# The four running sums of a Strassen pair move into four PSUM tiles, with weight buffers of their own

## The chip, the cores and the metric

The kernel runs on one core of one Trainium2 chip. The metric is the device time of one execution in microseconds; the number for a kernel is the median of its runs.

## The reference, cut to what matters

The reference computes one step of a two-layer decoder for 512 prompt tokens and 64 sample tokens (576 columns, kept transposed: features on the partitions, tokens along the free dimension). Each layer is a mixer with an input and an output projection, then a squared-ReLU MLP, then a gated embedding. The change touches the MLP of the second layer, and through shared PSUM space the stages on both sides of it:

```python
def channel_mixer(h, norm_g, w_up, w_down):
    a = jax.nn.relu(rmsnorm(h, norm_g) @ w_up)
    return h + (a * a) @ w_down
```

with `w_up` 1024 x 4096 and `w_down` 4096 x 1024, all in float32.

## The kernel before, in words

**Products.** A weight arrives as a unit of 128 x 512 floats (256 KB, four 128 x 128 blocks). ScalarE rounds it to a high part (`whi`, a cast, L92), VectorE takes the rest (`wlo`, a subtraction, L93); activations are split likewise. A product is then three matmuls of 128 x 288 columns: high by high, high by low, low by high. 576 columns make two halves of 288, `lo` and `hi`. `pieces` (L128) is the plain linear map: 24 matmuls for each unit and both halves, into a PSUM tile `[128, 2, 512]` of the pool `big`.

**The MLP of the second layer** is `ffn_quad` (L305). Its 32 output tiles of the up projection are made as four `plain` ones (L336) and 14 `pair`s (L344). A pair makes two tiles at once by a Strassen scheme (Winograd's form): seven products of 12 matmuls in place of eight, into four running sums X, Z, Y and V. Their order is the tuple `plan` in `quad` (L175): X from b11, Z from t1, Y from t2, again X from b21, again Y from t3, V from t4, again Z from b22. The operands t1 to t4 are sums of activations, made once by `operands` (L317) while the plain tiles run; the sums of weights (`qsum`, L160) are made on VectorE for each pair. Between the products VectorE and ScalarE read the running sums: `L350` copies X, `L352` reads Y, `L354` reads X again, `L356` reads Y again, `L357` and `L361` read Z, `L359` reads V. Each pair's results go through ReLU, square and a scale, and are split into `hidh` and `hidl`. After every two pairs eight `back` products (L370, "down" in the trace, 24 matmuls each) add their part of the down projection to the residual h on VectorE (L372); while the pairs j run, the downs of the two before are made, four to a pair.

**PSUM.** `banks(3, 2)` (L63) opens a pool of three `big` tiles and two small ones, from the second norm of layer 0 to the end. A pair takes two `big` tiles: X and Y are the halves of one, `qa`, Z and V those of the other, `qb`:

```python
al = self.big.tile([128, 2, 512], F32, name="qa", tag="big")
be = self.big.tile([128, 2, 512], F32, name="qb", tag="big")
X, Y, Z, V = al[:, 0, 0:HT], al[:, 1, 0:HT], be[:, 0, 0:HT], be[:, 1, 0:HT]
```

**Buffers in SBUF.** All splits of weights, for pairs and for everything else, come from one ring of three `whi` and three `wlo`. Raw weights of a pair (`qraw`) have eight buffers, their sums four.

**What sets the order.** Nothing is ordered by hand at these places. The program is written in the order of the functions above; a scheduler then orders each engine's instructions and sets a semaphore wait wherever two instructions of different engines touch the same tile. Each engine takes its list strictly in that order; loads of weights wait in the list of SyncE.

Of the kernel before, what the change touches and what calls it, by code (L numbers as in the profile page):

```python
# [6 lines left out]
F32 = mybir.dt.float32  # L7
# [9 lines left out]
HT = 288  # L17
KU = 4
NTS = [128, 603]
QRAW, QSUM, PLAIN = 8, 4, 2  # L20
EPS = 1e-6
# [11 lines left out]
def f(ap):  # L33
    return ap.bitcast(F32)
# [7 lines left out]
class Net:  # L42
# [43 lines left out]

    def split_unit(self, raw):
        nc, kt = self.nc, raw.shape[1]
        ps = [128, KU, 128]
        hi = self.wp.tile([128, kt, 128], F32R, name="whi", tag="whi", padded_shape=ps)  # L90
        lo = self.wp.tile([128, kt, 128], F32R, name="wlo", tag="wlo", padded_shape=ps)
        nc.scalar.copy(hi, raw)  # L92
        self.lo.tensor_sub(lo, raw, f(hi))  # L93
        return hi, lo
# [52 lines left out]
    def quad_units(self, s1, s2):  # L147

        nc = self.nc
        ps = [128, KU, 128]  # L150
        n = s1.shape[1] // 2
        raws = []
        for s, a in ((s1, 0), (s2, 0), (s2, n), (s1, n)):
            raw = self.qp.tile(ps, F32, name="qraw", tag="qraw", bufs=QRAW)
            self.last = nc.sync.dma_start(raw, s[:, a:a + n])
            self.flush(self.share)
            raws.append(raw)
        a11, a21, a22, a12 = raws

        def add(a, b):  # L160
            o = self.qp.tile(ps, F32, name="qsum", tag="qsum", bufs=QSUM)
            nc.vector.tensor_add(o, a, b)
            return o

        yield a11
        u1 = add(a21, a22)
        yield u1
        u2 = add(u1, a11)
        yield u2
        yield a12  # L170
        yield add(a11, a21)
        yield a22
        yield add(u2, a12)

    def quad(self, s1, s2, B):  # L175


        al = self.big.tile([128, 2, 512], F32, name="qa", tag="big")
        be = self.big.tile([128, 2, 512], F32, name="qb", tag="big")
        X, Y, Z, V = al[:, 0, 0:HT], al[:, 1, 0:HT], be[:, 0, 0:HT], be[:, 1, 0:HT]  # L180
        mm = self.nc.tensor.matmul
# [3 lines left out]
        for o, b, first in plan:  # L185
            hi, lo = self.split_unit(next(us))
            n = len(B[b])
# [8 lines left out]
    def split(self, x, pool=None, tag="x"):  # L196
# [3 lines left out]
        lo = pool.tile([128, T], F32R, name=tag + "l", tag=tag + "l")  # L200
        self.nc.scalar.copy(hi, x)
        self.nc.vector.tensor_sub(lo, x, f(hi))
        return hi, lo
# [101 lines left out]
def ffn_quad(N, h, xs, up, down, after, psrc, gain):  # L305
# [3 lines left out]
    with tc.tile_pool(name="qw", bufs=2, reuse_waits="tile") as qp, \  # L309
# [3 lines left out]
        N.quad_pools(qp)  # L313
        lo, hi = slice(0, HT), slice(HT, T)
        B = {n: [] for n in ("b11", "b21", "b22", "t1", "t2", "t3", "t4")}

        def operands(k):  # L317
# [11 lines left out]
            ph, pl = N.split(p, qx, "qx")  # L329
            qh, ql = N.split(q, qx, "qx")  # L330
            cut = lambda t, s: (t[0][:, s], t[1][:, s])
            for n, t, s in (("b11", xs[k], lo), ("b21", xs[k + 4], lo), ("b22", xs[k + 4], hi), ("t1", (ph, pl), lo),
# [11 lines left out]
        def pair(m):  # L344
            s = ft.tile([128, 2, HT], F32, name="qs", tag="qs")
            a = ft.tile([128, T], F32, name="fa", tag="fa")
            b = ft.tile([128, T], F32, name="fb", tag="fs")
            g = N.quad(up[m], up[m + 1], B)
            X = next(g)
            nc.scalar.copy(s[:, 0], X)  # L350
            Z, Y = next(g), next(g)
            nc.vector.tensor_sub(s[:, 1], s[:, 0], Y)  # L352
            next(g)
            nc.scalar.activation(a[:, lo], X, AF.Relu)  # L354
            next(g)
            nc.vector.tensor_sub(s[:, 0], s[:, 0], Y)  # L356
            nc.vector.scalar_tensor_tensor(b[:, hi], Z, -1.0, s[:, 0], op0=MUL, op1=SUB)  # L357
            V = next(g)
            nc.vector.tensor_sub(b[:, lo], V, s[:, 0])  # L359
            next(g)  # L360
            nc.vector.tensor_add(a[:, hi], Z, s[:, 1])  # L361
            nc.scalar.activation(b, b, AF.Relu)
# [14 lines left out]
        for j in range(16):  # L377
# [7 lines left out]
            else:  # L385
                hid[j // 2] += pair(2 * j)
            if j == 15:
# [1332 lines left out]
def trunk(tc, I, O):  # L1720
    with ExitStack() as ctx:
# [19 lines left out]
        with N.banks(2, 4):  # L1741
# [13 lines left out]
            xs = N.norm_end(acc)  # L1755
            layer0(N, h, xs, I, O, V, lambda m: N.norm_tile(h[m], col("norm_ffn0", m)))
        ctx.enter_context(N.banks(3, 2))
        xs = N.norm_end()
        with tc.tile_pool(name="s5pre", bufs=1, reuse_waits="tile") as pool:
            pre = s5_pre(N, pool, I, D)  # L1760
            p = ffn(N, h, xs, I["up0"], I["down0"], lambda m: N.norm_tile(h[m], col("norm_pe0", m)), I["p0"],
                    lambda: (next(pre, None), next(pre, None)))
            for _ in pre:
                pass
        xs = N.norm_end()
        N.norm_begin()
        pe(N, h, xs, I["gate0"], I["proj0"], p, lambda m: N.norm_tile(h[m], col("norm_mix1", m)), True)
        xs = N.norm_end()
        layer1(N, h, xs, I, O, V, D, lambda m: N.norm_tile(h[m], col("norm_ffn1", m)))
        xs = N.norm_end()  # L1770
        p = ffn_quad(N, h, xs, I["up1"], I["down1"], lambda m: N.norm_tile(h[m], col("norm_pe1", m)), I["p1"],
                     lambda m: col("norm_ffn1", m))
        xs = N.norm_end()
# [42 lines left out]
```

## Time and profile before

| | |
|---|---|
| median of 3 runs | 1589.25 us (1587.27 to 1590.63) |
| the profiled execution's own time | 1587.57 us |
| its span | 1585.8 us |
| TensorE busy | 1473.8 us, 93% |
| VectorE busy | 951.5 us, 60% |
| ScalarE busy | 593.6 us, 37% |

The profiled execution took 1.8 us more than its span, and 1.7 us less than the median. TensorE is the engine that the others feed. Its matmuls overlap each other, so its busy time hides short stops; how far the starts of matmuls lie apart tells more than their lengths. The pairs of `ffn_quad` fill the span from 1084.56 to 1468.09 us.

### The profile page before, as it was taken

Reading aid. Unit: us, or ns where it says so; the run is one execution under the profiler, and the core shown is the slowest. Engines: PE = TensorE matmul, PEld = TensorE weight load, DVE = VectorE, ACT = ScalarE, POOL = GpSimd, SP = SyncE. Lnnn points to the kernel's source line nnn. Section 1 sums busy time; section 2 is a strip of 40 time slices with the busy share of each in tenths; the row PEclk is TensorE's granted clock in tenths of the full one; section 3 lists DMA queues with packets and bytes.
Section 4 is the critical chain, followed back from the end, with each engine's and each line's share of the span. In section 5 each row is a group of like instructions: output and inputs, shape, how many; then the busy total and the mean of one; then the engine's idle time right before and its main releaser. Section 6 shows DMA issues by size and latency. Waiting matters only on the chain. (4 is left out here: it accounts for less than half of the span.)

```text
span 1585.8 us, 27284 instructions
## 1 busy us (share of the span) xinstructions
PE 1473.8 (93%) x10687; PEld 1428.8 (90%) x10687; DVE 951.5 (60%) x1680; ACT 593.6 (37%) x1121; POOL 430.2 (27%) x689
## 2 busy tenths in 40 slices
PE   7999999998989899999999997998989899998996
PEld 6889899788989899999999987997989888898996
DVE  6757455589834224454336785677666666665655
ACT  5462363223222112223334512544434343444552
POOL 4644253234868544510111151020000000000212
PEclk9998999999989999999999996997999999999998
DMA  5121112252322333363222754341222222221222
GB/s 195 57 74 48 38 54 84 89 151 68 122 75 91 95 102 102 100 174 105 81 76 80 256 149 130 91 133 54 80 74 81 80 80 68 80 75 39 78 85 73
DMA packets 107281, 149.46 MB, mean 94 GB/s; under 512 B 30800, under 2 KB 46544, under 8 KB 107152
## 3 DMA queue, kind: packets, MB, share of 16 engines
q1 hardware_dynamic: 78960, 128.63, 26.1%
q10 hardware_dynamic: 27616, 16.99, 3.9%
q8 instruction: 84, 1.38, 0.4%
q0 software_dynamic: 576, 2.10, 0.3%
q14 instruction: 45, 0.37, 0.1%
HBM read 130.73 MB, written 16.43 MB: 93 GB/s over the span
## 5 line engine op out<-in xcount | busy, mean ns | idle before, releaser
L92 ACT CAST whi<-wraw 128x512 fp32r<-128x512 f32 (+2 forms) x352 | 211.8, 605 | 531.9 <-PE down L121 142.8
L93 DVE TENSOR_TENSOR wlo<-wraw,whi 128x512 fp32r<-128x512 f32 (+1 forms) x306 | 222.7, 729 | 200.8 <-ACT whi L92 194.2
L120 PE MATMUL down<-hidh,whi 128*128 128x288 f32 x1024 | 306.2, 299 | 12.9 <-ACT whi L92 12.9
L122 PE MATMUL down<-hidh,wlo 128*128 128x288 f32 x1024 | 306.0, 299 | 0.0
L121 PE MATMUL down<-hidl,whi 128*128 128x288 f32 x1024 | 303.2, 296 | 0.0
L228 POOL TENSOR_TENSOR acc<-acc,sq 128x576 f32<-128x576 f32 x45 | 69.0, 1533 | 747.7 <-ACT sq L227 729.4
L120 PEld LDWEIGHTS down<-hidh,whi 128*128 128x128 f32 x1024 | 194.7, 190 | 16.5 <-ACT whi L92 16.5
L121 PEld LDWEIGHTS down<-hidl,whi 128*128 128x128 f32 x1024 | 195.9, 191 | 0.0
L122 PEld LDWEIGHTS down<-hidh,wlo 128*128 128x128 f32 x1024 | 193.9, 189 | 0.2 <-DVE wlo L93 0.2
L120 PE MATMUL up<-xh,whi 128*128 128x288 f32 x576 | 172.7, 300 | 8.2 <-ACT whi L92 8.0
L122 PE MATMUL up<-xh,wlo 128*128 128x288 f32 x576 | 171.8, 298 | 2.5 <-DVE wlo L93 2.5
L121 PE MATMUL up<-xl,whi 128*128 128x288 f32 x576 | 172.1, 299 | 0.7 <-DVE xl L215 0.7
L120 PEld LDWEIGHTS up<-xh,whi 128*128 128x128 f32 x576 | 109.6, 190 | 9.3 <-ACT whi L92 9.1
L122 PEld LDWEIGHTS up<-xh,wlo 128*128 128x128 f32 x576 | 109.9, 191 | 3.8 <-DVE wlo L93 3.7
L121 PEld LDWEIGHTS up<-xl,whi 128*128 128x128 f32 x576 | 109.8, 191 | 1.4 <-DVE xl L215 1.3
L93 POOL TENSOR_TENSOR wlo<-wraw,whi 128x512 fp32r<-128x512 f32 x46 | 61.0, 1326 | 105.0 <-ACT whi L92 91.2
L120 PE MATMUL gate<-xh,whi 128*128 128x288 f32 x256 | 75.6, 295 | 0.0
L121 PE MATMUL gate<-xl,whi 128*128 128x288 f32 x256 | 75.5, 295 | 0.0
L122 PE MATMUL gate<-xh,wlo 128*128 128x288 f32 x256 | 75.4, 294 | 0.0
L372 DVE TENSOR_TENSOR h<-h,down 128x576 f32<-128x576 f32 x64 | 48.2, 754 | 44.6 <-PE down L122 44.6
L92 ACT CAST whi<-qsum 128x512 fp32r<-128x512 f32 x56 | 34.7, 620 | 99.2 <-PE down L121 59.4
L93 DVE TENSOR_TENSOR wlo<-qsum,whi 128x512 fp32r<-128x512 f32 x56 | 38.6, 688 | 38.1 <-ACT whi L92 38.0
(630 smaller groups left out, 3825.9 us busy)
## 6 DMA issues: line engine op xcount, KB each, us to landing
wraw<-in_down SPq DMA_DIRECT2D x128, 256.0 KB, 2.7
wraw<-in_up SPq DMA_DIRECT2D x72, 256.0 KB, 2.6
qraw<-in_up SPq DMA_DIRECT2D x56, 256.0 KB, 2.6
wraw<-in_wA SPq DMA_DIRECT2D x48, 256.0 KB, 2.6
wraw<-in_wout SPq DMA_DIRECT2D x32, 256.0 KB, 2.6
wraw<-in_gate SPq DMA_DIRECT2D x32, 256.0 KB, 2.6
S<-in_S SPq DMA_DIRECT2D x8, 512.0 KB, 3.9
wraw<-in_wcd SPq DMA_DIRECT2D x16, 256.0 KB, 4.0
```

The source lines that it names most:

```text
L92: nc.scalar.copy(hi, raw)
L93: self.lo.tensor_sub(lo, raw, f(hi))
L120: mm(o, hi, xh[:, s], start=start, stop=False)
L121: mm(o, hi, xl[:, s], start=False, stop=False)
L122: self.pe_last = mm(o, lo, xh[:, s], start=False, stop=stop)
L228: nc.gpsimd.tensor_add(self.acc, self.acc, sq)
L372: nc.vector.tensor_add(c3(h[m]), c3(h[m]), ps)
```

## The change

The four sums get a PSUM tile each from the small pool, and for the length of `ffn_quad` the pools are two `big` tiles and four small ones (`banks(2, 4)`), so that the downs have two `big` tiles to themselves. The splits of a pair's weights get a ring of three of their own (`qhi`, `qlo`, QW = 3). The sums of weights are made in place, in two `qsum` buffers and in the raw buffer of a21; raw buffers go from eight to six. The results of a pair are made in place in `fa` and `fb`, without the tile `qs`. The first pair is to be issued after the last operand splits (`begun`).

```diff
-QRAW, QSUM, PLAIN = 8, 4, 2
+QRAW, QSUM, QW, PLAIN = 6, 2, 3, 2
...
-    def split_unit(self, raw):
+    def split_unit(self, raw, pool=None, tag="w", bufs=None):
...
-        hi = self.wp.tile([128, kt, 128], F32R, name="whi", tag="whi", padded_shape=ps)
-        lo = self.wp.tile([128, kt, 128], F32R, name="wlo", tag="wlo", padded_shape=ps)
+        pool = pool or self.wp
+        hi = pool.tile([128, kt, 128], F32R, name=tag + "hi", tag=tag + "hi", padded_shape=ps, bufs=bufs)
+        lo = pool.tile([128, kt, 128], F32R, name=tag + "lo", tag=tag + "lo", padded_shape=ps, bufs=bufs)
...
-        u1 = add(a21, a22)
-        yield u1
-        u2 = add(u1, a11)
-        yield u2
+        u = self.qp.tile(ps, F32, name="qsum", tag="qsum", bufs=QSUM)
+        add(u, a21, a22)
+        yield u
+        add(u, u, a11)
+        yield u
         yield a12
-        yield add(a11, a21)
+        add(a21, a21, a11)
+        yield a21
         yield a22
-        yield add(u2, a12)
+        add(u, u, a12)
+        yield u
...
-        al = self.big.tile([128, 2, 512], F32, name="qa", tag="big")
-        be = self.big.tile([128, 2, 512], F32, name="qb", tag="big")
-        X, Y, Z, V = al[:, 0, 0:HT], al[:, 1, 0:HT], be[:, 0, 0:HT], be[:, 1, 0:HT]
+        one = lambda n: self.sm.tile([128, 512], F32, name=n, tag="sm")[:, 0:HT]
+        X, Z, Y, V = one("qx"), one("qz"), one("qy"), one("qv")
...
-            hi, lo = self.split_unit(next(us))
+            hi, lo = self.split_unit(next(us), self.qp, "q", QW)
...
-            nc.scalar.copy(s[:, 0], X)
+            nc.scalar.copy(b[:, lo], X)
             Z, Y = next(g), next(g)
-            nc.vector.tensor_sub(s[:, 1], s[:, 0], Y)
+            nc.vector.tensor_sub(a[:, hi], b[:, lo], Y)
...
-                hid[j // 2] += pair(2 * j)
+                with ExitStack() as c:
+                    if j == PLAIN:
+                        for x in begun:
+                            c.enter_context(tc.issue_after(x.ins))
+                    hid[j // 2] += pair(2 * j)
...
+        with N.banks(2, 4):
+            p = ffn_quad(N, h, xs, I["up1"], I["down1"], lambda m: N.norm_tile(h[m], col("norm_pe1", m)), I["p1"],
+                         lambda m: col("norm_ffn1", m))
         ctx.enter_context(N.banks(3, 2))
```

What this does to the engines' lists shows at three places. The first is VectorE at the end of layer 1, ahead of the second MLP: `gs` and `xl` belong to layer 1's gate, `outd` is its output projection, whose eight tiles are added to h. Before:

```order
L202 TENSOR_TENSOR xl<-gs,xh 128x576
L162 TENSOR_TENSOR qsum<-qraw 128x512
L162 TENSOR_TENSOR qsum<-qsum,qraw 128x512
L162 TENSOR_TENSOR qsum<-qraw 128x512
L1635 TENSOR_TENSOR h<-h,outd 128x576
L162 TENSOR_TENSOR qsum<-qsum,qraw 128x512
L93 TENSOR_TENSOR wlo<-wraw,whi 128x512
```

and now:

```order
L200 TENSOR_TENSOR xl<-gs,xh 128x576
L1638 TENSOR_TENSOR h<-h,outd 128x576
L94 TENSOR_TENSOR wlo<-wraw,whi 128x512
L1638 TENSOR_TENSOR h<-h,outd 128x576
L94 TENSOR_TENSOR wlo<-wraw,whi 128x512
```

The four sums of the first pair's weights no longer stand among the adds of layer 1; they come after the operands, some 80 rows later.

The second place is TensorE in the middle of a pair, where the second product into X (from `xh`, `xl`) ends. Before:

```order
L191 MATMUL qa<-xl,whi 128x288
L192 MATMUL qa<-xh,wlo 128x288
L190 MATMUL qa<-qxh,whi 128x288
L191 MATMUL qa<-qxl,whi 128x288
L192 MATMUL qa<-qxh,wlo 128x288
```

and now:

```order
L190 MATMUL qx<-xl,qhi 128x288
L191 MATMUL qx<-xh,qlo 128x288
L121 MATMUL down<-hidh,whi 128x288
L122 MATMUL down<-hidl,whi 128x288
L123 MATMUL down<-hidh,wlo 128x288
```

The second product into Y used to follow at once; now 12 matmuls of a down stand between the two, and a down's 24 matmuls stand within the pair's second product.

The third place is TensorE where the last plain tile (`up`) ends. Before, the first pair begins there:

```order
L120 MATMUL up<-xh,whi 128x288
L121 MATMUL up<-xl,whi 128x288
L122 MATMUL up<-xh,wlo 128x288
L190 MATMUL qa<-xh,whi 128x288
L191 MATMUL qa<-xl,whi 128x288
```

and now:

```order
L121 MATMUL up<-xh,whi 128x288
L122 MATMUL up<-xl,whi 128x288
L123 MATMUL up<-xh,wlo 128x288
L121 MATMUL down<-hidh,whi 128x288
L122 MATMUL down<-hidl,whi 128x288
```

The first two downs, whose first 12 matmuls need only the first two plain tiles, come ahead of the first pair and are then woven into it.

## Rows read from the trace of the kernel before

**Rows 1.** The page, part 1: busy time, share of span, instructions.

```profile
PE 1473.8 (93%) x10687; PEld 1428.8 (90%) x10687; DVE 951.5 (60%) x1680; ACT 593.6 (37%) x1121; POOL 430.2 (27%) x689
```

**Rows 2.** Windows by stage: length; busy PE, PEld, DVE, ACT, POOL; PEclk, DMA, GB/s.

```profile
1027.60:1058.02 30.42, 27.62 (x195) 26.95 (x194) 23.59 (x30) 16.94 (x28) 9.31 (x6) 0.94 0.48 154
1058.02:1084.56 26.54, 26.54 (x198) 26.33 (x197) 23.48 (x40) 14.63 (x27) 2.54 (x2) 1.00 0.24 75
1084.56:1123.14 38.58, 32.18 (x182) 29.37 (x181) 26.23 (x45) 14.91 (x25) 0.00 (x0) 0.78 0.17 55
1123.14:1450.68 327.54, 299.85 (x2162) 289.27 (x2161) 214.13 (x335) 132.99 (x228) 0.00 (x0) 1.00 0.24 75
1450.68:1468.09 17.41, 15.35 (x111) 14.47 (x110) 9.98 (x17) 7.88 (x14) 0.00 (x0) 1.00 0.10 31
1468.09:1503.28 35.19, 35.19 (x267) 35.19 (x265) 22.97 (x34) 18.57 (x29) 7.87 (x6) 1.00 0.25 80
```

**Rows 3.** Waits of PE, 1123 to 1468: total us, times, longest.

```profile
PE qa L190 <- ACT fa L354: 11.6, 13, 0.9
PE qa L190 <- DVE qs L352: 10.1, 13, 0.8
PE down L120 <- ACT whi L92: 8.1, 13, 0.6
```

**Rows 4.** Timeline of PE in one pair: start, us, instruction, [idle before <-releaser].

```profile
1264.27 0.29 PE L192 MATMUL qa<-qxh,wlo 128*128 128x288 f32 x1
1265.36 0.40 PE L190 MATMUL qa<-xh,whi 128*128 128x288 f32 x1 [0.80 <-DVE qs L352]
...
1268.10 0.40 PE L190 MATMUL qa<-qxh,whi 128*128 128x288 f32 x1 [0.89 <-ACT fa L354]
...
1270.59 0.40 PE L120 MATMUL down<-hidh,whi 128*128 128x288 f32 x1 [0.62 <-ACT whi L92]
```

**Rows 5.** Timeline of DVE and ACT in the same pair.

```profile
1264.86 0.45 DVE L352 TENSOR_TENSOR qs<-qs,qa 128x288 f32<-128x288 f32 x1
...
1267.64 0.40 ACT L354 ACTIVATE fa<-qa 128x288 f32<-128x288 f32 x1
1269.92 0.62 ACT L92 CAST whi<-wraw 128x512 fp32r<-128x512 f32 x1 [1.87 <-issue]
```

**Rows 6.** Timeline of DVE and PE, then a wait of PE, end of layer 1.

```profile
1036.96 0.69 DVE L162 TENSOR_TENSOR qsum<-qraw 128x512 f32<-128x512 f32 x1 [4.63 <-DMA qraw<-in_up]
...
1039.79 0.37 PE L120 MATMUL outd<-xh,whi 128*128 128x288 f32 x1 [1.93 <-DVE h L1635]
...
PE outd L121 <- DVE xl L202: 0.3, 1, 0.3
```

**Rows 7.** Timeline of DVE around the first pair.

```profile
1083.12 0.51 DVE L325 SCALAR_TENSOR_TENSOR qt<-h,vec,qb 128x288 f32<-128x288 f32 x1
1083.55 0.45 DVE L326 TENSOR_TENSOR qt<-qb 128x288 f32<-128x288 f32 x1
1083.92 0.69 DVE L162 TENSOR_TENSOR qsum<-qraw 128x512 f32<-128x512 f32 x1
1084.52 0.75 DVE L202 TENSOR_TENSOR qxl<-qt,qxh 128x576 fp32r<-128x576 f32 x1
```

**Rows 8.** Windows (as Rows 2) and timeline of PE within the first pair.

```profile
1086.20:1090.87 4.67, 2.12 (x12) 1.61 (x12) 4.67 (x10) 2.26 (x4) 0.00 (x0) 1.00 0.15 56
1090.87:1107.94 17.07, 13.37 (x52) 11.44 (x51) 10.52 (x18) 4.70 (x8) 0.00 (x0) 0.52 0.15 46
...
1106.48 0.44 PE L120 MATMUL down<-hidh,whi 128*128 128x288 f32 x1
1106.72 0.44 PE L121 MATMUL down<-hidl,whi 128*128 128x288 f32 x1
```

**Rows 9.** Groups by form, ACT, 1123 to 1468: busy us, mean ns.

```profile
L92 ACT CAST whi<-qraw 128x512 fp32r<-128x512 f32 x38 | 23.5, 618 | 25.3 <-PE qa L191 25.3
```

**Rows 10.** The page, part 6: loads of a pair's weights, KB, median us to landing.

```profile
qraw<-in_up SPq DMA_DIRECT2D x56, 256.0 KB, 2.6
```

More of the change, by code (lines that the diff above doesn't have):

```diff
@@ L158, in quad_units @@
         a11, a21, a22, a12 = raws
[L160 to L163, printed above, removed]
+        add = nc.vector.tensor_add
         yield a11
-        u1 = add(a21, a22)
-        yield u1
-        u2 = add(u1, a11)
-        yield u2
+        u = self.qp.tile(ps, F32, name="qsum", tag="qsum", bufs=QSUM)
[3 more added lines that the diff above has]
+        yield u
         yield a12
-        yield add(a11, a21)
+        add(a21, a21, a11)
+        yield a21
         yield a22
-        yield add(u2, a12)
+        add(u, u, a12)
+        yield u
     def quad(self, s1, s2, B):
-        al = self.big.tile([128, 2, 512], F32, name="qa", tag="big")
-        be = self.big.tile([128, 2, 512], F32, name="qb", tag="big")
-        X, Y, Z, V = al[:, 0, 0:HT], al[:, 1, 0:HT], be[:, 0, 0:HT], be[:, 1, 0:HT]
+        one = lambda n: self.sm.tile([128, 512], F32, name=n, tag="sm")[:, 0:HT]
+        X, Z, Y, V = one("qx"), one("qz"), one("qy"), one("qv")
         mm = self.nc.tensor.matmul
@@ L200, in split @@
         lo = pool.tile([128, T], F32R, name=tag + "l", tag=tag + "l")
-        self.nc.scalar.copy(hi, x)
-        self.nc.vector.tensor_sub(lo, x, f(hi))
+        self.split_last = (self.nc.scalar.copy(hi, x), self.nc.vector.tensor_sub(lo, x, f(hi)))
         return hi, lo
@@ L314, in ffn_quad @@
         lo, hi = slice(0, HT), slice(HT, T)
+        begun = []
         B = {n: [] for n in ("b11", "b21", "b22", "t1", "t2", "t3", "t4")}
@@ L330, in operands @@
             qh, ql = N.split(q, qx, "qx")
+            begun[:] = N.split_last
             cut = lambda t, s: (t[0][:, s], t[1][:, s])
@@ L344, in pair @@
         def pair(m):
-            s = ft.tile([128, 2, HT], F32, name="qs", tag="qs")
             a = ft.tile([128, T], F32, name="fa", tag="fa")
@@ L355, in pair @@
             next(g)
-            nc.vector.tensor_sub(s[:, 0], s[:, 0], Y)
-            nc.vector.scalar_tensor_tensor(b[:, hi], Z, -1.0, s[:, 0], op0=MUL, op1=SUB)
+            nc.vector.tensor_sub(b[:, lo], b[:, lo], Y)
+            nc.vector.scalar_tensor_tensor(b[:, hi], Z, -1.0, b[:, lo], op0=MUL, op1=SUB)
             V = next(g)
-            nc.vector.tensor_sub(b[:, lo], V, s[:, 0])
+            nc.vector.tensor_sub(b[:, lo], V, b[:, lo])
             next(g)
-            nc.vector.tensor_add(a[:, hi], Z, s[:, 1])
+            nc.vector.tensor_add(a[:, hi], Z, a[:, hi])
             nc.scalar.activation(b, b, AF.Relu)
@@ L1756, in trunk @@
             layer0(N, h, xs, I, O, V, lambda m: N.norm_tile(h[m], col("norm_ffn0", m)))
-        ctx.enter_context(N.banks(3, 2))
[L1758 to L1772, printed above, removed]
+        with N.banks(3, 2):
+            xs = N.norm_end()
+            with tc.tile_pool(name="s5pre", bufs=1, reuse_waits="tile") as pool:
+                pre = s5_pre(N, pool, I, D)
+                p = ffn(N, h, xs, I["up0"], I["down0"], lambda m: N.norm_tile(h[m], col("norm_pe0", m)), I["p0"],
+                        lambda: (next(pre, None), next(pre, None)))
+                for _ in pre:
+                    pass
+            xs = N.norm_end()
+            N.norm_begin()
+            pe(N, h, xs, I["gate0"], I["proj0"], p, lambda m: N.norm_tile(h[m], col("norm_mix1", m)), True)
+            xs = N.norm_end()
+            layer1(N, h, xs, I, O, V, D, lambda m: N.norm_tile(h[m], col("norm_ffn1", m)))
+            xs = N.norm_end()
+        with N.banks(2, 4):
+            p = ffn_quad(N, h, xs, I["up1"], I["down1"], lambda m: N.norm_tile(h[m], col("norm_pe1", m)), I["p1"],
+                         lambda m: col("norm_ffn1", m))
+        ctx.enter_context(N.banks(3, 2))
         xs = N.norm_end()
```

## Prediction

> **What bounds the kernel now.** The page first: TensorE (PE) is busy for 93% of the span [rows 1], so a change is worth the time in which PE stands still, and no more. Windows by stage show where that is [rows 2]. The yardstick is the stage from 1468.09, the last downs: 264 matmuls (72 left of the last pair's downs, 192 of the last eight) in 35.19 us at clock 1.00, without a stop. So matmuls can start every 35.19 / 264 = 0.1333 us. The count x267 in the window takes in neighbours; I use the program's counts.
>
> Steady pairs: from 1123.14 to 1450.68 twelve pairs begin, 327.54 / 12 = 27.30 us each [rows 2]. A pair is 7 x 12 products and 4 x 24 down matmuls, 180 x 0.1333 = 24.00 us. So **3.30 us of each pair is lost**. The last pair has 84 + 24 matmuls before the long run of downs, 14.40 us, and takes 17.41: 3.01 lost. Together 12 x 3.30 + 3.01 = **42.6 us**.
>
> The waits name the loss [rows 3]: three kinds, 13 times each, 29.8 us. The list shows less than 42.6 because a stop is counted from the modelled end of the last matmul. By starts the stop at 1265.36 comes 1.09 us after the start before it, 0.96 too late [rows 4], and the matmul after a stop starts 0.24 later instead of 0.13.
>
> Who is waited for? At 1265.36 a matmul into X waits for L352, which reads Y; at 1268.10 one into Y waits for L354, which reads X [rows 4, 5]. Neither touches what the matmul writes: X and Y are halves of one tile, and the wait is for the tile. At 1270.59 a down waits for its weight cast, which began at 1269.92 [rows 5]. That row names no releaser; by the program the cast takes its buffer, from the ring of three that pairs and downs share, from the pair's second Y product, which ends just then.
>
> Two more places lose time. At the end of layer 1 VectorE (DVE) stands 4.63 us at a sum of the first pair's weights, whose load has not landed; behind it in the list are the adds of `outd`, and PE waits for one of them [rows 6]. That stage is 192 matmuls, 25.6 us, in 30.42: 4.8 lost [rows 2]. And the first pair takes 38.58 in place of 24.0 [rows 2]: DVE is busy making operands and plain results, PE makes only 12 matmuls in 4.67 us, then its clock falls to 0.52 for 17.07 us [rows 8].
>
> **The change part by part.** The sum is made against the profiled execution's own 1587.57 us.
>
> *Steady pairs.* Seven products, four downs, seven casts, seven splits, four sums and the same reads of the sums remain: 24.00 us of PE. Busy DVE is 214.13 / 12 = 17.8 us for a pair and ScalarE (ACT) 132.99 / 12 = 11.1 [rows 2], so neither bounds a 24.0 us pair. What can stop PE is lateness in a list, so I laid the new PE order on a time axis at 0.1333 a matmul, from a pair's first X product: b11 to 1.6, t1 to 6.4 (a down's 24 in between), t2 to 8.0, b21 to 9.6, half a down, t3 11.2 to 12.8, V 12.8 to 14.4, most of a down, b22 16.5 to 18.1, downs to 24.0. Then the old waits' places, with 0.25 us for a hand-over (a product's last matmul lasts 0.29, 0.16 more than its step [rows 4], and the matmul that waited for L354 starts 0.06 after its end [rows 4, 5]):
> - t3 into Y needs L352's successor, after t2 at 8.0: behind one split it is done by 8.7. Needed at 11.2, spare 2.5.
> - b21 into X needs only the copy of X: one 0.62 cast and the 0.4 copy after 1.6, by 2.8. Needed at 8.0.
> - b22 into Z needs two reads of 0.45 after t3, by 14.0. Needed at 16.5, spare 2.5.
> - the cast for t3 waits in its own ring for t1's end at 6.4, and takes 0.62 [rows 9]: 7.3. Needed at 11.2.
> - a down needs its `big` tile back from the down two before. The tightest: a down ends at 20.8, DVE has splits and two other rows ahead of its add and is done by 23.6; the tile is needed at 25.9, spare 2.3.
> - a raw weight in six buffers: the third load of the next pair can issue once the in-place sum has read a11, at -2.5, lands 2.6 later [rows 10], and is first read at 19.3.
>
> So all 42.6 should go, and the spares above are what protects it: **-42.6**, bounds -42.6 and, if a wait of the old size returns in each pair at one place or at two, -28 or -14 (rivals 1 and 3).
>
> On the waits of rows 3 the Trainium skill bears (PSUM — Partial Sum Buffer, PSUM bank collisions raise a hardware error): PSUM is to be guarded by bank and quadrant, because two engines in one bank collide. By that page's 512 floats to a bank, X and Y had a bank each already, so the two waits guarded nothing the chip needs, and separate tiles may drop them; were the tile wait a bank's, the sum would be that of the third rival below. No run here shows banks.
>
> *End of layer 1.* The four sums leave DVE's list there. 4.8 us were lost, of which a wait for a split of the gate's result stays (0.3 idle [rows 6], some 0.5 with its restart). What else could bind: DVE has an add, a split and a norm row for each 3.2 us tile, 2.2 us at the lengths of the like shapes in rows 7. **-4.3**, bounds 0 (another row of DVE stops it as long) and -4.8.
>
> *First pair.* PE now has a down ahead of it. Its `big` tile, one of two, must first be read by the third plain tile's L339, which in the new DVE list stands behind the split of a down's weights, whose cast waits for a buffer that PE gives back only at the end of the fourth plain tile. So after PE's last plain matmul come, in a row: hand-over 0.25, cast 0.62, split 0.60, two operand rows of 0.43 and one of 0.37, L339 0.75 (the length of L202, of the same shape), hand-over [rows 7, 9]: about **3.5 us in which PE stands still**. The fourth plain tile's L339 follows behind two splits, two operand rows and one more of 0.67 (3.5 us in all with itself), against 14 matmuls, 1.9 us: 1.6 more. After that DVE has 6.9 us of rows for 10.9 us of matmuls, and PE is not waiting. 24.0 + 5.1 = 29.1 at full clock. The clock fell in the old order when PE did 12 matmuls in 4.67 us [rows 8]; the new order does 14 in the first 7, so I expect it to fall here too. At the low level matmuls start 0.24 apart [rows 8], 0.107 more. For a low stretch of 6.8 us (28 matmuls) that is 3.0: 32.1 against 38.58. **-6.5**, bounds -9.5 (no fall) and -1.9 (17 us low again, 71 matmuls, 7.6).
>
> *The rest.* The plain tiles run without stops at present (26.54 us at clock 1.00) and keep their order but for the norm factor, which comes 14 matmuls earlier. After the last down the pools change back, and the first gate tile takes space that pairs have left long ago: 0.
>
> Sum: -42.6 - 4.3 - 6.5 = -53.4, so 1587.57 - 53.4 = **1534.2**; the median of the runs shown lies 1.7 higher than this execution, so a median of 1534 to 1536. I give 1534.5.
>
> **The rivals.**
> 1. *A new wait in every pair.* With three own buffers and sums in place, a late row on DVE (busy 17.8 of 24.0, 74% instead of 65%) takes back more than the 2.3 to 2.5 us spare. The price is like that of a cast waited for now, 8.1 + restarts over 13 pairs, about 1.1 each: 1534.5 + 14 = **1549**. For it: DVE's list is strict and mixes three jobs. Against: three spares would have to be wrong.
> 2. *The first pair stays as it is*, because operands on DVE set its length and the clock stays low: 1534.5 + 6.5 = **1541**. For it: DVE is busy 4.67 of 4.67 us where PE starves [rows 8]. Beside it the Trainium skill (TensorE: Matmul & The Clock Gate, HAM oscillation): gaps between bursts of matmuls bring the clock down. Rows 8 agree: the clock fell after such gaps.
> 3. *The two tile waits stay*, only the cast's goes: by starts they cost 0.96 and, with its idle time 0.09 longer [rows 4], 1.05, each with 0.10 for the restart: 2.2 x 13 = 29, **1563**. Against: in the new list 12 matmuls of other work stand between.
> 4. *Slower.* Six raw buffers instead of eight make a load late in each pair: DVE stops at the in-place sum as it did at 1036.96, 4.63 us [rows 6], and PE with it: 13 x 4.63 = 60, **1595**. It decides against the change from 53.4 / 13 = 4.1 us a pair. Against: a load lands in 2.6 us [rows 10] and has some 20 us.
>
> **How the numbers follow.** Forecast 0.68, rivals 0.14, 0.12, 0.04 and 0.02. The forecast's own range is 1528 (no fall of the clock, all of layer 1's loss and the shorter half of the first pair's stops gone) to 1543 (17 us low, half of layer 1's stop stays, 0.15 us a pair). Rival 1 lies at 1549 and may be somewhat dearer, so the range reaches to 1552: **1528 to 1552**, which leaves out rivals 3 and 4 and the ends. Within 0.2% is about what this measurement cannot tell from no change. Faster 0.96; same 0.01 and slower 0.03, from rival 4 and what I have not seen.
>
> **What would show it.** Right: pairs 24.0 us apart; no PE wait on the reads of another sum or on a down's cast in that stage; no stop of DVE for `qraw` at the end of layer 1; one PE stop of some 3.5 us at the first down, waiting for L339, and a lower clock soon after. Wrong: a PE wait of about a microsecond once a pair (rival 1 or 3, by the row waited for), DVE standing for `qraw` in steady pairs (4), or a first pair near 38 us (2).

## The result

The changed kernel takes **1531.82 us** (median of 4 runs, 1528.98 to 1535.03) against 1588.26 us before (4 runs, 1586.44 to 1590.63): a ratio of 0.9644, 95% interval 0.9616 to 0.9673. The forecast was 1534.5, its range 1528 to 1552. The medians lie 56.4 us apart. The profiled execution took 1534.25 us, and its span is 1532.4 us in place of 1585.8: the stages below are those of this execution, one of the two longer ones of the four.

### The profile page after: what moved, and what is told of

It is laid out like the page before. It is cut to its first block, busy times and chain, and to the rows that moved or that the text cites. A ratio compares the mean times of both kernels' runs of the same rounds, so it can differ in the third digit from the quotient of the medians.

```text
span 1532.4 us, 27273 instructions
## 1 busy us (share of the span) xinstructions
PE 1454.0 (95%) x10687; PEld 1422.4 (93%) x10687; DVE 944.6 (62%) x1680; ACT 593.0 (39%) x1121; POOL 429.4 (28%) x689
## 4 chain that ended last, share of the span: by engine, by line
PE 73%; DVE 13%; POOL 7%; issue 3%; ACT 3%; DMA 1%; ACTq 1%; SPq 0%; DVEq 0%; POOLq 0%
PE down L123 9%; PE down L121 8%; PE down L122 8%; PE up L121 2%; PE gate L121 2%; PE gate L123 2%; PE up L123 2%; PE gate L122 2%; PE up L122 2%; PE pp L535 2%; DVE Y L721 1%; DVE wlo L94 1%; POOL s5x L1351 1%; POOL s5x L1348 1%; POOL s5y L1352 1%
## 5 line engine op out<-in xcount | busy, mean ns | idle before, releaser
L93 ACT CAST whi<-wraw 128x512 fp32r<-128x512 f32 (+2 forms) x352 | 211.7, 605 | 490.3 <-PE down L122 176.1
L94 DVE TENSOR_TENSOR wlo<-wraw,whi 128x512 fp32r<-128x512 f32 (+1 forms) x306 | 219.5, 719 | 194.5 <-ACT whi L93 187.7
L121 PE MATMUL down<-hidh,whi 128*128 128x288 f32 x1024 | 304.7, 298 | 7.6 <-ACT whi L93 4.3
L123 PE MATMUL down<-hidh,wlo 128*128 128x288 f32 x1024 | 305.6, 299 | 0.0
L121 PEld LDWEIGHTS down<-hidh,whi 128*128 128x128 f32 x1024 | 194.4, 190 | 8.1 <-ACT whi L93 4.5
L123 PEld LDWEIGHTS down<-hidh,wlo 128*128 128x128 f32 x1024 | 194.2, 190 | 0.0
L121 PE MATMUL up<-xh,whi 128*128 128x288 f32 x576 | 172.3, 299 | 8.1 <-ACT whi L93 7.8
L123 PE MATMUL up<-xh,wlo 128*128 128x288 f32 x576 | 171.8, 298 | 2.4 <-DVE wlo L94 2.4
L121 PEld LDWEIGHTS up<-xh,whi 128*128 128x128 f32 x576 | 109.1, 189 | 9.2 <-ACT whi L93 9.0
L123 PEld LDWEIGHTS up<-xh,wlo 128*128 128x128 f32 x576 | 109.6, 190 | 3.8 <-DVE wlo L94 3.6
L94 POOL TENSOR_TENSOR wlo<-wraw,whi 128x512 fp32r<-128x512 f32 x46 | 60.9, 1325 | 105.3 <-ACT whi L93 94.7
L121 PE MATMUL gate<-xh,whi 128*128 128x288 f32 x256 | 75.6, 295 | 0.0
L123 PE MATMUL gate<-xh,wlo 128*128 128x288 f32 x256 | 75.6, 295 | 0.0
L371 DVE TENSOR_TENSOR h<-h,down 128x576 f32<-128x576 f32 x64 | 48.0, 749 | 39.6 <-PE down L123 39.6
L121 PE MATMUL qkv<-xh,whi 128*128 128x288 f32 x192 | 60.3, 314 | 0.8 <-ACT whi L93 0.8
L122 PE MATMUL qkv<-xl,whi 128*128 128x288 f32 x192 | 59.3, 309 | 0.0
```

Source lines behind the costliest of these rows:

```text
L121: mm(o, hi, xh[:, s], start=start, stop=False)
L122: mm(o, hi, xl[:, s], start=False, stop=False)
L123: self.pe_last = mm(o, lo, xh[:, s], start=False, stop=stop)
L371: nc.vector.tensor_add(c3(h[m]), c3(h[m]), ps)
```

## The profile after

Line numbers have moved by one to three: the weight cast is L93 now, its split L94, the linear matmuls L121 to L123, those of a pair L189 to L191, the residual add L371. The page, part 1, answers to [rows 1]:

```profile
PE 1454.0 (95%) x10687; PEld 1422.4 (93%) x10687; DVE 944.6 (62%) x1680; ACT 593.0 (39%) x1121; POOL 429.4 (28%) x689
```

TensorE (PE) runs the same number of instructions, with 19.8 us less busy time and 53.4 less span. A matmul right after a stop is longer (0.40 us against 0.29 in [rows 4]) and so is one at the low clock (0.44 in [rows 8]), so some of the lost time had counted as busy.

Windows of the changed kernel by stage (columns as in [rows 2]): layer 1's output projection, the plain tiles, the first pair, the next twelve pairs, the same twelve with the last pair and all the downs behind them, and the rest of the program:

```profile
1030.34:1056.43 26.09, 25.84 (x195) 25.61 (x194) 21.20 (x26) 16.49 (x28) 9.04 (x6) 1.00 0.45 144
1056.43:1083.19 26.76, 26.76 (x198) 26.31 (x196) 24.98 (x41) 15.25 (x28) 2.68 (x2) 1.00 0.27 83
1083.19:1113.64 30.45, 26.95 (x182) 26.48 (x181) 25.68 (x45) 13.84 (x23) 0.00 (x0) 0.89 0.25 81
1113.64:1397.25 283.61, 283.61 (x2138) 283.61 (x2137) 208.95 (x340) 134.37 (x231) 0.00 (x0) 1.00 0.29 88
1113.64:1449.95 336.31, 336.31 (x2534) 336.31 (x2533) 241.31 (x388) 159.69 (x272) 7.85 (x6) 1.00 0.27 84
1449.95:1532.40 82.45, 68.50 (x498) 66.60 (x496) 46.15 (x76) 34.93 (x57) 16.64 (x15) 0.94 0.25 79
```

In the fourth and fifth row PE is busy for the whole length of the stage. Against [rows 2]: the output projection 26.09 in place of 30.42, the plain tiles 26.76 in place of 26.54, the first pair 30.45 in place of 38.58; the pairs and last downs 336.31 in place of 327.54 + 17.41 + 35.19 = 380.14. That is -4.3, +0.2, -8.1 and -43.8, from the start of the first stage to the end of the last -56.1. The output projection starts 2.7 us later than before, after work that the change does not touch; over all profiles shown here that start lies between 1026 and 1031.

The waits of PE from 1030 to 1114 (total us, times, longest) are all that is left; from 1114 to 1451 there is none, where [rows 3] had 39:

```profile
PE down L121 <- ACT qxh L200: 3.3, 1, 3.3
PE outd L122 <- DVE xl L200: 0.3, 1, 0.3
PE qx L189 <- ACT qhi L93: 0.2, 1, 0.2
```

The one stop, on the timeline of PE, ACT and DVE after the last plain matmul (start, us, instruction, idle time and releaser):

```profile
1083.05 0.29 PE L123 MATMUL up<-xh,wlo 128*128 128x288 f32 x1
1083.30 0.62 ACT L93 CAST whi<-wraw 128x512 fp32r<-128x512 f32 x1 [1.48 <-issue]
1083.95 0.69 DVE L94 TENSOR_TENSOR wlo<-wraw,whi 128x512 fp32r<-128x512 f32 x1 [0.76 <-ACT whi L93]
1084.56 0.51 DVE L327 SCALAR_TENSOR_TENSOR qt<-h,vec,qt 128x288 f32<-128x288 f32 x1
1084.98 0.51 DVE L324 SCALAR_TENSOR_TENSOR qt<-h,vec,qb 128x288 f32<-128x288 f32 x1
1085.10 1.47 ACT L200 CAST qxh<-qt 128x576 fp32r<-128x576 f32 x2 [1.19 <-DVE qt L327]
1085.41 0.45 DVE L325 TENSOR_TENSOR qt<-qb 128x288 f32<-128x288 f32 x1
1085.78 0.75 DVE L339 TENSOR_TENSOR fa<-up,r 128x576 f32<-128x576 f32 x1
1086.68 0.58 PE L121 MATMUL down<-hidh,whi 128*128 128x288 f32 x1 [3.33 <-ACT qxh L200]
```

This is the row of work that the prediction laid out: cast, split, three operand rows, the plain tile's read L339, then the down. The trace names the cast of `qxh` as releaser, which ended at 1086.57; L339 ended at 1086.53. A down reads nothing of `qxh`; the experiment on the plain read settles which it was. The clock fell within the stop, 0.85 us before its end, to 0.50 (1.2 of 2.4 GHz), and stayed there for 6.83 us. A window of that stretch:

```profile
1085.83:1092.66 6.83, 5.81 (x23) 5.50 (x24) 6.79 (x13) 3.06 (x5) 0.00 (x0) 0.50 0.11 38
```

## The experiments

**The theories.** The prediction gave each stop in a pair a cause of its own: two waits for a tile, which separate tiles lift, and one for a cast, which a ring of its own lifts. If so, the parts add up, and a kernel with one part alone keeps the other's stops. The rival: the stops have a common condition, and one part removes them all.

The table gives for each kernel two stages read from starts of matmuls: `outd` is layer 1's output projection (192 matmuls, 25.6 us at 0.1333), MLP the second MLP from its first up matmul to its last down matmul (2904 matmuls, 387.2 us). A pair is the mean of ten, from the end of b22 in the third pair to that in the thirteenth. Medians are of all runs shown for the kernel. The ratio, with its 95% interval, is to the runs of the kernel before that go with each kernel (medians 1587.39 to 1588.26) and not the quotient of two medians of this table. Stages and pairs are those of each kernel's profiled execution.

| kernel | median us (range) | ratio | outd | MLP | a pair |
|---|---|---|---|---|---|
| before | 1588.26 | | 30.41 | 445.13 | 27.29 |
| changed | 1531.82 (1528.98 to 1535.03) | 0.9644 [0.9616, 0.9673] | 26.09 | 393.39 | 23.89 |
| tiles, no ring | 1536.32 (1534.94 to 1538.19) | 0.9678 [0.9658, 0.9697] | 26.09 | 397.78 | 24.03 |
| ring, no tiles | 1538.67 (1533.25 to 1541.57) | 0.9690 [0.9658, 0.9723] | 26.09 | 400.20 | 24.02 |
| neither | 1581.77 (1577.38 to 1582.17) | 0.9952 [0.9934, 0.9970] | 26.09 | 441.33 | 27.06 |
| before, with tiles | 1536.98 (1534.20 to 1538.35) | 0.9679 [0.9659, 0.9699] | 27.85 | 395.92 | 24.02 |
| six splits in turn | 1556.84 (1552.73 to 1557.27) | 0.9797 [0.9779, 0.9815] | 26.12 | 414.96 | 25.29 |
| two sums to a tile | 1541.67 (1539.19 to 1545.14) | 0.9712 [0.9690, 0.9735] | 26.09 | 403.62 | 23.95 |
| before, first-pair rule | 1581.69 (1579.59 to 1585.81) | 0.9968 [0.9950, 0.9987] | 26.09 | 443.61 | 27.27 |
| before, in place | 1583.15 (1579.34 to 1589.61) | 0.9991 [0.9970, 1.0011] | 27.01 | 445.40 | 27.10 |
| no first-pair rule | 1533.14 (1530.58 to 1533.94) | 0.9656 [0.9637, 0.9675] | 28.29 | 391.74 | 23.89 |
| plain read first | 1531.34 (1529.08 to 1532.45) | 0.9643 [0.9621, 0.9666] | 26.09 | 392.37 | 23.89 |
| first operands | 1531.52 (1527.59 to 1532.80) | 0.9639 [0.9620, 0.9658] | 26.10 | 393.12 | 23.89 |

### Tiles without the ring

```diff
-            hi, lo = self.split_unit(next(us), self.qp, "q", QW)
+            hi, lo = self.split_unit(next(us))
```

> The changed kernel, but the pairs' weights are again split into the three whi and wlo buffers that everything else uses; four PSUM tiles, sums in place and the late first pair stay. In the new list of TensorE the products of a pair follow each other again, with 2 down matmuls before the last product and 70 after it, much as in the kernel before. Theory (tile waits cost 2.2 us a pair and the shared ring 1.1): only the stop at the down's cast returns, 13 x 1.1 = 14 us, so about 1546 us, and TensorE waits once a pair for a whi cast and never for a read of another sum. Rival A (the PSUM tiles do it all, the ring nothing): 1532. Rival B (the ring does it all, by letting downs stand between the products): all 42 us return, 1574.

Measured: 1536.32, a pair in 24.03 us: 10 us under the theory's 1546, 4 above rival A's 1532. PE's only two waits from 1080 to 1455:

```profile
PE qx L189 <- ACT whi L93: 4.5, 1, 4.5
PE qx L191 <- DVE wlo L94: 1.5, 1, 1.5
```

Both are in the first pair. The wait of a down for its cast, once a pair in [rows 3], did not come back, although pairs and downs share three buffers as before.

### The ring without the tiles

```diff
-        one = lambda n: self.sm.tile([128, 512], F32, name=n, tag="sm")[:, 0:HT]
-        X, Z, Y, V = one("qx"), one("qz"), one("qy"), one("qv")
+        al = self.big.tile([128, 2, 512], F32, name="qa", tag="big")
+        be = self.big.tile([128, 2, 512], F32, name="qb", tag="big")
+        X, Y, Z, V = al[:, 0, 0:HT], al[:, 1, 0:HT], be[:, 0, 0:HT], be[:, 1, 0:HT]
...
-        with N.banks(2, 4):
```

> The changed kernel, but X and Y, and Z and V, are halves of two big tiles again, out of three; own weight ring, sums in place and the late first pair stay. In the new list downs stand between most products (8 matmuls between the second and third, 24 between the two that met at the second old stop). Theory (a tile wait costs what is not covered): the cast stop is gone (14 us), the gains at the end of layer 1 and in the first pair stay (12), the second tile stop is covered by 24 matmuls, the first by 8 of them in part, 0.3 us a pair; but with two of three big tiles in a pair's hands a down that follows a down waits for its add, about 1 us, once or twice a pair: 1588 - 26 - 29 + 4 + 13 to 26 = 1550 to 1563 us. Rival B (the ring does it all): 1532 to 1536. Rival C (the tile waits stay whole): 1562, with the waits of TensorE on the reads of the other half, 13 times each.

Measured: 1538.67, a pair in 24.02 us: under the theory's 1550 to 1563, 3 us above the range of rival B. PE's waits from 1078 to 1455:

```profile
PE qa L190 <- ACT qhi L93: 7.8, 1, 7.8
PE qa L192 <- DVE qlo L94: 1.1, 1, 1.1
PE down L122 <- DVE hidl L201: 0.4, 1, 0.4
```

The first two are in the first pair. X and Y are halves of one tile again, yet no wait for a read of the other half is left. Each of the two parts by itself removes all three stops: the additive theory fell.

### The tiles alone, put into the kernel before

The edit is the diff's four tiles and `banks(2, 4)`, nothing else.

> The kernel before with the four PSUM tiles and the pools of two big and four small tiles alone; weight ring shared, sums not in place, first pair not held back. Theory: the two tile waits go, 13 x 2.2 = 29 us, the cast stop, the stop at the end of layer 1 and the long first pair stay: 1559 us. Rival A (tiles do it all): 1546 (42 us). Rival B (ring does it all): 1588.

Measured: 1536.98, 22 us under the theory's 1559 and 9 under rival A's 1546, and the same as tiles without the ring: outd and MLP together take 423.77 us here and 423.87 there. Sums in place, fewer raw buffers and the rule for the first pair together add nothing to the tiles.

### Neither tiles nor ring

Both edits above in one kernel. A new theory stood behind this run and the next: a wait costs only the time that no other matmul fills, and it is the downs that can fill it.

> The changed kernel without its four tiles and without its own ring: sums in halves of two big tiles, pools of three and two as before, split weights from the common ring; sums and results in place, six raw buffers and the rule for the first pair stay. TensorE's order in a pair is that of the kernel before. Theory (tiles or ring, either lifts all three stops, and nothing else does): the three stops are back in every pair, 27.0 to 27.3 us a pair, and the rule for the first pair gives its 5 to 7 us: 1577 to 1583. Rival (sums in place or the rule have a part in what tiles alone and ring alone gave): 24 to 25.5 us a pair, 1536 to 1560.

Measured: 1581.77, a pair in 27.06 us, as the theory has it. The waits of PE from 1120 to 1460:

```profile
PE qa L190 <- ACT fa L354: 11.5, 13, 0.9
PE down L121 <- ACT whi L93: 8.4, 13, 0.9
PE qa L190 <- DVE fa L352: 7.2, 13, 0.6
```

The three kinds of [rows 3], 13 times each. This closes a square whose four kernels differ in tiles and ring alone; outd and MLP together: neither 467.4, tiles 423.9, ring 426.3, both 419.5. The first part, whichever it is, brings 41 to 44 us, the second 4 to 7. Of those 4 to 7 the steady pairs have 0.13 to 0.14 us each, 1.8 in all; the rest lies in the first pair, where PE's waits add up to 6.0 us with the tiles alone, 8.9 with the ring alone and 3.5 with both.

The tiles bring the downs a second big tile of their own as well. Halves of two tiles with that second tile and the shared ring were not run, so that it has no part in the tiles' 44 us is argued: two of the three waits are for reads of the sums, which no tile of the downs lifts, and the run below lets downs move with the pools as before.

### Six splits in turn

Why the order of the program does this is seen in how one pair's products (180 matmuls, a pair in the steady part) are laid out on TensorE. X, Z, Y, V stand for the products in the order of `plan`, "down" for matmuls of downs:

```
neither            X12 Z12 Y12 X12 Y12 down2 V12 down22 Z12 down72
six in turn        X12 Z12 Y12 down23 X12 down1 Y12 down28 V12 down25 Z12 down19
ring, no tiles     X12 (old pair's Z12 between) Z12 down12 Y12 down12 X12 down24 Y12 down28 V12 down20
                   (in every other pair down16 Y12 down8)
tiles, no ring     X2 down24 X10 Z12 Y12 X12 V2 Y12 V10 down2 Z12 down70
changed            X12 Z2 down24 Z10 Y12 X12 down12 Y12 V12 down16 Z12 down44
```

Splits take buffers in the order in which the program is written: seven for a pair, then its downs. With three in common, the first down's split, the eighth, takes the buffer of the fifth product (the second into Y), so none of the pair's own downs can stand before that product's end, and the row "neither" has none among the first five. With six in common it would be the second product's. The kernel keeps the halves of two big tiles, and lets pairs and downs take in turn a buffer of the pairs' ring and one of the common ring:

```diff
+    def turn(self, name):
+        self.n = getattr(self, "n", 0) + (name in ("q", "down"))
+        return (self.qp, "q", QW) if name in ("q", "down") and hasattr(self, "qp") and self.n % 2 else ()
...
-        return self.split_unit(self.load_unit(src, kt))
+        return self.split_unit(self.load_unit(src, kt), *self.turn(name))
...
-            hi, lo = self.split_unit(next(us), self.qp, "q", QW)
+            hi, lo = self.split_unit(next(us), *self.turn("q"))
...
```

> The changed kernel, but the sums are halves of two big tiles again with three big tiles and two small ones, and pairs and downs share their split buffers: each takes in turn one of the pairs' ring of three and one of the common ring of three, so that six splits in the order of the program are in flight. The order on TensorE has 23 downs between the second product of Y's first turn and b21, but a single down between b21 and t3. Theory (what the tile wait costs is decided by what stands between the two products, and the downs can stand there once a down's split need not wait for the pair's own): the wait for the second read of X is left, 0.9 to 1.15 us for each of 13 pairs, 12 to 15 us above the kernel with a ring of its own (1538.7): 1549 to 1554. Rival (a ring of the pairs' own is what counts): three stops again, 1575 to 1582. Rival (six buffers are enough whatever the order): 1535 to 1540.

Measured: 1556.84, a pair in 25.29 us. One kind of wait is left from 1110 to 1460, and the timeline shows it with a single down ahead of it:

```profile
PE qa L194 <- ACT fa L358: 9.1, 12, 0.8
...
1226.25 0.29 PE L196 MATMUL qa<-xh,qlo 128*128 128x288 f32 x1
1226.38 0.29 PE L127 MATMUL down<-hidh,qlo 128*128 128x288 f32 x1
1226.98 0.40 ACT L358 ACTIVATE fa<-qa 128x288 f32<-128x288 f32 x1
1227.43 0.40 PE L194 MATMUL qa<-qxh,whi 128*128 128x288 f32 x1 [0.75 <-ACT fa L358]
```

L358 is the second read of X (L354 before). Where 23 downs stand between the products, the wait for the read of Y does not show; where one stands, the wait is there, 1.05 us from start to start, in each of twelve pairs. This is the theory's forecast in kind; the time lies 3 us above its range. The wait with its restart is 1.0 us of the 1.3 that a pair loses; the rest is a second short stop at a down, 0.37 us from start to start (1221.53 to 1221.90 in the same pair), too short for the list of waits. So the tile wait is real with the halves, and costs the time that nothing fills.

### Two sums to a tile in their own pool

X with Y and Z with V in tiles of two banks, the downs with two big tiles to themselves, own ring kept.

```diff
-        one = lambda n: self.sm.tile([128, 512], F32, name=n, tag="sm")[:, 0:HT]
-        X, Z, Y, V = one("qx"), one("qz"), one("qy"), one("qv")
+        def two(n):
+            t = self.sm.tile([128, 2, 512], F32, name=n, tag="sm")
+            return t[:, 0, 0:HT], t[:, 1, 0:HT]
+
+        X, Y = two("qa")
+        Z, V = two("qb")
...
-        with N.banks(2, 4):
+        N.smw = 2
+        with N.banks(2, 2):
...
```

`smw` gives the norm's small tile the same width for this stage.

> The changed kernel, with X and Y as halves of one tile of two banks and Z and V of another, taken from the small pool as two tiles of two banks, so that the downs keep two big tiles; everything else as in the changed kernel. Theory: a wait for a read of the other half returns wherever too little other work stands between; in the new list 24 down matmuls stand before most second products, so part of it is covered and 5 to 20 us return: 1537 to 1552 us, with waits of TensorE on the reads of X or Y (L351, L353) or of Z or V. If the waits were of no account: 1532. If they return whole: 1561.

Measured: 1541.67, a pair in 23.95 us. The time lies in the theory's range, 1537 to 1552, but not by the theory's cause: the steady pairs lose nothing, and from 1100 to 1460 only one wait, of 0.7 us, is on a read of a sum (`PE qa L194 <- DVE fb L360`). What this kernel loses against the changed one lies at the ends, in the second and third pair and above all after the last product, where no downs were left to fill (timeline of PE):

```profile
1431.78 0.29 PE L196 MATMUL qb<-xh,qlo 128*128 128x288 f32 x1
1435.33 0.85 PE L122 MATMUL down<-hidh,whi 128*128 128x288 f32 x2 [3.26 <-ACT hidh L205]
```

### The first-pair rule and the sums in place, each alone in the kernel before

The first is the diff's `begun` with `issue_after`, the second its sums and results in place with six raw buffers.

> The kernel before with that rule alone. Theory: the end of layer 1 loses its stop (4.3 us); the first pair still stands right behind the plain tiles on TensorE and has no downs ahead, so it gains little, 0 to 4: 1580 to 1584 us; the steady pairs keep 27.3 us. Rival (the rule alone makes both gains): 1576.

> The kernel before with the sums of weights and the pair's results in place and six raw buffers alone. Theory (in place costs and gains nothing in steady pairs): 1588 us, within 3; the first pair's order moves a little and with it one or two us. Rival (in place brings part of the gain): 1580 or less. Rival (the smaller buffers cost and the other parts pay for it): 1592 or more.

Measured: 1581.69, in the theory's range, and 1583.15, 2 us under it, with an interval that reaches over 1: no gain can be told there. The rule takes the output projection from 30.41 to 26.09 us, so the sums of weights in VectorE's list there were the cause of [rows 6]. Sums in place shorten it too, to 27.01: VectorE still stands 3.7 us for the load, but PE waits only 0.4 us for an add of `outd`, in place of 1.9. Neither changes a pair by more than 0.2 us.

### The changed kernel without the first-pair rule

```diff
-                with ExitStack() as c:
...
-                    hid[j // 2] += pair(2 * j)
+                hid[j // 2] += pair(2 * j)
```

> The changed kernel without the rule that the first pair is issued after the last operand splits. In the lists the first pair's products follow the last plain tile at once again, and VectorE makes the first pair's sums early. Theory (this rule alone made the gains at the end of layer 1 and in the first pair): 4 us return at the end of layer 1, with a stop of VectorE for qraw, and 6 to 9 in the first pair: 1542 to 1545 us. Rival (the gains come with the tiles and the ring): 1532.

Measured: 1533.14, as the rival has it. The output projection takes 2.2 us more, and PE waits from 1026 to 1450 at new places (`ss` is the sum of squares of the norm):

```profile
PE ss L260 <- POOL acc L226: 2.4, 1, 2.4
PE qy L189 <- ACT qxh L200: 1.2, 1, 1.2
PE outd L121 <- DVE h L1634: 0.8, 1, 0.8
PE up L121 <- ACT whi L93: 0.6, 1, 0.6
```

In exchange the stop at the first down and the low clock are gone: the products stand first again, and VectorE begins the first pair's sums at 1034.0, in the changed kernel at 1090.71. In the last experiment below the products stand first too, with the sums from 1076.8 on, and a stop of 2.5 us stays, so the early sums have a part in it. The two orders cost the same to 0.6 us: 420.0 against 419.5 for both stages.

### The plain tile's read first

```diff
-            a = ft.tile([128, T], F32, name="fa", tag="fa")
-            nc.vector.tensor_mul(c3(a), ps, N.r3)
+            r3 = N.r3
+            with tc.high_priority():
+                a = ft.tile([128, T], F32, name="fa", tag="fa")
+                nc.vector.tensor_mul(c3(a), ps, r3)
```

> The changed kernel with the read of a plain tile's sums (L339) ahead of everything else on VectorE. Theory (TensorE's one stop of 3.3 us waits for the third plain tile's L339, not for the ScalarE cast that the trace names): the stop goes or shrinks below 1 us, the clock does not fall after it, 3.5 + 0.7 (6.8 us at the low level, partly waiting anyway) to 6 us less: 1526 to 1528 us. Rival (the wait is for the cast of an operand, as the trace names it): the stop stays, 1532.

Measured: 1531.34, no gain that can be told, where the theory had 1526 to 1528 and a stop below 1 us. The timeline of PE and DVE (L341 is the plain read):

```profile
1082.79 0.69 DVE L94 TENSOR_TENSOR wlo<-wraw,whi 128x512 fp32r<-128x512 f32 x1 [0.75 <-ACT whi L93]
1083.39 0.75 DVE L341 TENSOR_TENSOR fa<-up,r 128x576 f32<-128x576 f32 x1
1084.29 0.37 PE L121 MATMUL down<-hidh,whi 128*128 128x288 f32 x1 [2.10 <-DVE fa L341]
...
1087.27 0.76 DVE L341 TENSOR_TENSOR fa<-up,r 128x576 f32<-128x576 f32 x1
1088.17 0.37 PE L121 MATMUL down<-hidh,whi 128*128 128x288 f32 x1 [2.05 <-DVE fa L341]
```

This settles it: the cast of `qxh` starts at 1084.61 here, after the down, and the first down waits for the plain tile's read. The theory had the wait right and its price wrong. The read came forward by three operand rows and the stop shrank from 3.49 to 2.27 us (beyond a step); in exchange a stop of 2.22 us for the fourth tile's read appeared, which the changed kernel does not have.

### The first pair after the first operands

```diff
-            begun[:] = N.split_last
+            if k == 0:
+                begun[:] = N.split_last
```

> The changed kernel, but the first pair need only be issued after the first operands' splits, not the last ones'. VectorE's list at the end of layer 1 keeps the order of the changed kernel, and TensorE's first pair begins with its products, X and half of Z, with downs behind them. Theory (the stop at the first down is only the plain tile's read standing late): no stop of 3.5 us after the plain tiles, outd stage 26.1 us, second MLP 390 to 391.5 us in place of 393.4, 1528 to 1530. Rival (the operands on VectorE and ScalarE set the first pair's length, the stop only moves to a product): 393 us or more, 1532 to 1534.

Measured: 1531.52, MLP 393.12 us, as the rival has it. The stop moved from the first down to a product (waits of PE from 1020 to 1460), while VectorE was busy without a gap (window of the first 10 us after the plain tiles):

```profile
PE qy L189 <- ACT qxh L200: 2.5, 1, 2.5
...
1081.91:1091.91 10.00, 6.63 (x39) 5.72 (x38) 10.00 (x20) 4.16 (x7) 0.00 (x0) 0.92 0.32 105
```

## Why the prediction was right, and where its reasons were not

**Steady pairs** (forecast -42.6, measured -43.8). The yardstick, 180 matmuls without a stop, was right; the rest is that matmuls start 0.1327 us apart here (23.89 / 180). The spare of the old waits held: in a steady pair L351, the read of Y, starts at 1285.92 and takes 0.45, and the product that needs it starts at 1288.90, 2.5 us later, as worked out. One spare was misread: the working had the third raw weight of the next pair first read 19 us after landing. In the trace VectorE reads it the moment it lands, with no spare at all (waits of DVE, 1083 to 1450, and one of them; this load was issued at 1270.41):

```profile
DVE qsum L164 <- DMA qraw<-in_up: 4.4, 11, 0.5
1273.02 0.69 DVE L164 TENSOR_TENSOR qsum<-qraw 128x512 f32<-128x512 f32 x1 [0.37 <-DMA qraw<-in_up]
```

That is the sign that the prediction had given for rival 4, VectorE standing for `qraw` in steady pairs. It cost nothing here: no PE wait followed.

What was wrong is the account by cause. "Two waits for a tile, one for a cast" reads as three prices with an edit each. The runs show one condition with two parts: a tile wait, and nothing to put into it, because the downs' splits stood in the same ring behind the pair's. The third stop hung on the tile as well. With separate tiles and the shared ring, V's last ten matmuls stand between the Y product that frees the cast's buffer and the down, and cover the cast's 0.62 us; with halves, two downs come ahead of V. That V is held back there by the read of Z in its own tile follows from the program, but was not tried alone. Rival 3 (1563) priced the two tile waits as if nothing could fill them. That fits "neither", and no kernel in which downs can move; "six splits in turn" shows the price where they fill one of the two places and not the other.

Of the rule on PSUM in the Trainium skill (PSUM — Partial Sum Buffer, PSUM bank collisions raise a hardware error) the prediction said that X and Y had a bank each, so that waits between them guarded nothing. The trace agrees as far as it goes: separate tiles ran without these waits, halves of one tile with them (1.05 us from start to start).

**End of layer 1** (forecast -4.3, measured -4.3). Right in mechanism and size; the wait of 0.3 us that was to stay did. The kernel before with the rule alone shows the cause. Part of the 4.8 us lost there was a low clock (0.94 in [rows 2], 1.00 now), which the prediction did not price by itself.

**First pair** (forecast -6.5, measured -8.1). The first stop was forecast at 3.5 us and took 3.49 from start to start beyond a step, the low stretch at 6.8 and took 6.83. The second stop, 1.6 us for the read of the fourth plain tile, is the term that was wrong: it did not come (timeline of PE, DVE and ACT):

```profile
1089.37 0.75 DVE L339 TENSOR_TENSOR fa<-up,r 128x576 f32<-128x576 f32 x1
1089.40 0.61 ACT L93 CAST qhi<-qraw 128x512 fp32r<-128x512 f32 x1
1090.07 0.61 PE L189 MATMUL qx<-xh,qhi 128*128 128x288 f32 x1 [0.17 <-ACT qhi L93]
1090.47 0.44 PE L190 MATMUL qx<-xl,qhi 128*128 128x288 f32 x1
1090.71 0.44 PE L121 MATMUL down<-hidh,whi 128*128 128x288 f32 x1
```

The read ends at 1090.12, 0.59 us before the second down, which needs it, starts. At half clock the twelve matmuls ahead start 0.24 us apart and give the read that time; the working had the stop and the low clock beside each other as independent terms. What does stand there is a shorter wait that the working did not have, of the first product for its weight cast, 0.61 us from start to start. The low clock's term was off as well: 28 slow matmuls were counted for 6.8 us, but the clock fell within the stop, and 23 ran slow. From 1086.68 to 1092.79 those 23 took 6.11 us in place of 3.07 at a full step, 3.04 more, the cast's wait included. 23.89 + 3.49 + 3.04 = 30.4, against 30.45 measured.

**The sum.** The stages gave -56.1, the work before them +2.7, which the change does not touch. That the span's -53.4 equals the forecast's sum to a tenth is luck: 2.7 us of underestimate and 2.7 of a later start cancel in this execution. The medians, 56.4 apart, side with the stages.

## What to carry to other kernels

Price a wait by what can stand in its place: before giving each stop its own cause, ask what keeps other work from filling it, and try each part of a change alone and none, since two parts that each suffice look like one big gain that adds up. A ring of buffers handed out in program order decides from which product on later work can move up, and that can be counted without a run. When a stop moves and its length stays, as in the first pair, look for the engine that is busy throughout.

## What the runs showed of the hardware

The clock did not follow the length of a stop. In the changed kernel 6.83 us at half clock (0.50) came with one stop of 3.63 us from start to start. In the kernel with two sums to a tile the first down came after the same stop, 3.63 us, and the clock stayed at 1.00 (timeline of PE, then a window of that kernel from the stop's start):

```profile
1083.74 0.29 PE L124 MATMUL up<-xh,wlo 128*128 128x288 f32 x1
1087.37 0.37 PE L122 MATMUL down<-hidh,whi 128*128 128x288 f32 x1 [3.33 <-ACT qxh L205]
...
1083.74:1093.74 10.00, 5.11 (x37) 4.67 (x36) 9.21 (x17) 4.35 (x7) 0.00 (x0) 1.00 0.13 43
```

There it fell only after the last product, in the stop of 3.55 us shown above. With the plain read first there were two stops, 2.40 and 2.35 us, with twelve matmuls between, more lost in all than in the changed kernel, and the granted clock stayed at 1.00 too (window of that kernel):

```profile
1081.91:1091.91 10.00, 5.46 (x36) 4.57 (x35) 9.11 (x17) 4.41 (x8) 0.00 (x0) 1.00 0.13 41
```

At full clock that kernel's MLP was 1.0 us shorter (392.37 against 393.39) in spite of its second stop. So neither the length of a stop nor the sum of two decides by itself; what does, these runs do not show, and the low stretch in the changed kernel's profile need not be part of each of its executions.
